# Decaying keys and queries in place in the recurrence levels, and attention maxima in one pass

## The chip, the cores and the metric

The kernel runs on one core of a Trainium2 chip. The metric is the device time of one execution in microseconds. Three runs of the kernel before gave 2209.01, 2213.13 and 2214.48 us; the median is 2213.13.

## The reference

Two layers over 512 latent and 256 context tokens (768 columns in all), width 1024, all in float32. Each layer has three token mixers in parallel (pooling windows, attention with 8 query and 2 key heads, and a gated recurrence in both directions), a gated merge, an output projection and a feed-forward part. The change touches the recurrence and the maxima of the attention.

```python
def hgrn_scan(q, k, v, log_f, s0):
    # S_t = diag(f_t) S_{t-1} + k_t v_t^T,  o_t = S_t^T q_t,  k_t = 1 - f_t
    ...
    diff = G[:, :, :, None] - G[:, :, None, :]
    decay = jnp.exp(jnp.where(mask, diff, -jnp.inf))
    A = jnp.einsum('bnthk,bnshk,bntshk->bnhts', q, k, decay)
    o_intra = jnp.einsum('bnhts,bnshv->bnthv', A, v)
    ...

def _attend(q, k, v):
    s = jnp.einsum('bqhgd,bshd->bhgqs', q, k).astype(jnp.float32) * (HEAD_DIM ** -0.5)
    p = jax.nn.softmax(s, axis=-1).astype(v.dtype)
    return jnp.einsum('bhgqs,bshd->bqhgd', p, v)
```

Softmax does not change when the same number is taken from all scores of a row, so the maximum that is subtracted need not be exact.

## The kernel before, in words

Features lie on the 128 partitions and tokens along the columns, so a tile of one feature block is 128x768 (layer 0, all tokens) or 128x512 (layer 1, which needs outputs for latent tokens only). Large products are done in three matmuls, since each operand is split into a high and a low half (`load_w`, L243 for the low half of a weight; `gemm_h`, L261).

**The recurrence** (`hgrn`, L390 on) runs twice per layer, once for each pair of heads. It builds the decayed product of queries and keys inside chunks of 128 tokens level by level: `LEVELS` are the half-block lengths h = 1, 2, 4, ..., 64. At a level, the tokens of the two halves of each block of 2h see each other through the decay between them. Four state tiles, `Pf`, `Sf`, `Pb` and `Sb`, hold prefix and suffix products of the gates f in both directions. Per level:

- GpSimd forms the decayed keys `K` from the two directions (L436, L437), VectorE the decayed queries `Q` (L439, L440);
- TensorE (PE below) multiplies them per chunk and head (`scores`, L421) into PSUM tiles of the pool `pa`, tag `att`, of which there are four;
- VectorE copies the result under a mask into `AT` (L442);
- the states are extended to the next block length in place (L448), `Sf` and `Pb` on GpSimd, `Pf` and `Sb` on VectorE.

After the last level keys and queries are multiplied with the finished states, transposed, and summed into the chunk states `st`.

**The order.** PE's order is the order in which the program is written. Between two levels the program calls `fill(F)`: it takes work from a queue of generators (projections, pooling windows' products, gates and branch products of the merge, and in layer 0 the conditioning product `ada_group`, L173) until a credit of F microseconds is used. `PACE['hg']` holds F for both layers: 1.8 and 2.2. After each head pair `finish` empties what the next one needs, or all. The order of VectorE, ScalarE and GpSimd comes from a scheduler. Each call of `fill` also lets one step of the pooling windows onto VectorE (`windows`, L531 to L552).

**Attention** (`attn_max`, L599 on, and `attn_pv`). Row maxima come from an extra pass of scores per head: for each block of 128 queries a matmul with the high half `khh` of the keys and one with the low half `kll` (L618 for context keys, 256 columns; L626 for latent keys, 512 columns), and a reduction on VectorE (L619, L627). The pass of a head is spread over the value loop of the head before it; the first head of each of the two key heads has its pass ahead of that loop.

Of the kernel before, what the change touches and what calls it, by code (L numbers as in the profile page):

```python
# [39 lines left out]
PACE = {'hn': 3.5, 'gap': (6.4, 10.2), 'hg': (1.8, 2.2), 'att': (0.7, 0.24), 'head': (2.0, 0.6), 'mid': (1.0, 0.88), 'last': (1.0, 0.7), 'tail': (7.0, 5.0)}  # L40


class Trunk:
# [330 lines left out]
    def hgrn_proj(self, l, ws, full, hp, out):  # L374

        nc = self.nc
        c0 = 0 if full else LC
        for dirn in range(2):
            ps = yield from self.gemm_h(self.load_w(ws[dirn], [P, KD, P]), self.segs(True))
            k = self.t(hp, [P, T], F32, f"k{dirn}", bufs=2)  # L380
            for s0, s1, a in ps:
# [4 lines left out]
        for s0, s1, a in ps:
            nc.scalar.copy(q[:, s0:s1], a)
        out.append(q)

    def hgrn(self, l, p, kkq, full, hp, bo):  # L390
# [3 lines left out]
        F = PACE['hg'][l]  # L394

        kf, kb, q = kkq
        P_, S_ = {}, {}
        for dirn, k in ((0, kf), (1, kb)):
            f = self.t(hp, [P, T], F32, f"f{dirn}")
            e = self.t(hp, [P, T], F32, f"e{dirn}")  # L400
            if l > 0:
                col = dirn * 2 + p
                nc.vector.tensor_scalar(out=f, in0=k, scalar1=self.olb[:, 1, col:col + 1], scalar2=1.0, op0=ALU.mult, op1=ALU.add)
                nc.vector.tensor_scalar(out=k, in0=k, scalar1=self.olb[:, 0, col:col + 1], scalar2=0.0, op0=ALU.mult, op1=ALU.add)
            else:
                nc.vector.tensor_scalar(out=f, in0=k, scalar1=-1.0, scalar2=1.0, op0=ALU.mult, op1=ALU.add)
            nc.gpsimd.memset(e, 1.0)
            P_[dirn], S_[dirn] = (f if dirn == 0 else e), (e if dirn == 0 else f)
        Pf, Sf, Pb, Sb = P_[0], S_[0], P_[1], S_[1]

        AT = self.t(hp, [P, 2, NCH, P], F32, "AT")

        def scores(K, Q, evac):
            for g0 in range(ch0, NCH, 4):
                n = min(4, NCH - g0)
                pt = [self.t(self.pa, [P, 4, P], F32, "att") for _ in range(2)]
                for i in range(n):
                    sl = slice((g0 + i) * P, (g0 + i + 1) * P)
                    for hd in range(2):
                        ph = slice(64 * hd, 64 * hd + 64)  # L420
                        nc.tensor.matmul(pt[hd][:, i, :], K[ph, sl], Q[ph, sl], start=True, stop=True)  # L421
                for hd in range(2):
                    evac(AT[:, hd, g0:g0 + n], pt[hd][:, :n], n)


        K = self.t(hp, [P, T], F32, "K")
        nc.vector.tensor_add(K[:, c0:], kf[:, c0:], kb[:, c0:])
        self.fill(F + (PACE['gap'][l] if p else 0.0))
        scores(K, q, lambda o, i, n: nc.scalar.copy(o, i))
        self.fill(F)  # L430

        for li, h in enumerate(LEVELS):
            def half(X, e, s0=0):
                return X[:, s0:].rearrange("p (n e h) -> p n e h", e=2, h=h)[:, :, e, :]
# [28 lines left out]
        kts = [self.t(hp, [P, NCH, P], F32, "Q") for _ in range(2)]  # L463
# [3 lines left out]
        for dirn, src in ((0, Sf), (1, Pb)):  # L467
            for g in ((0, 4), (4, 5)) if dirn == 0 else ((3, 6), (0, 2)):
                pt = self.t(self.pa, [P, 4, P], F32, "att")
                n = g[1] - g[0]  # L470
                for i in range(n):
                    nc.tensor.transpose(pt[:, i, :], src[:, (g[0] + i) * P:(g[0] + i + 1) * P], self.ident)
                nc.scalar.copy(kts[dirn][:, g[0]:g[1], :], pt[:, :n, :])
            self.fill(1.2)
        for g in ((0, 2), (2, 4), (4, 5)):
            for dirn in range(2):
                order = orders[dirn]
                pt = self.t(self.pa, [P, 2, P], F32, "att")
                for i in range(*g):
                    nc.tensor.matmul(pt[:, i - g[0], :], kts[dirn][:, order[i], :], self.Vt[:, order[i], p * P:(p + 1) * P], start=True, stop=True)  # L480
# [24 lines left out]
        self.headnorm(on, o, c0, self.hnw[l], hp, "e0", "e1")  # L505
# [93 lines left out]
    def attn_max(self, hl, q, full, ap):  # L599
# [13 lines left out]
        for qi in range(c0 // P, NCH, 2):  # L613
            pc = self.t(self.pa, [P, 2, LC], F32, "att")
            for j in range(2):
                ql = s[:, (qi + j) * P:(qi + j + 1) * P]
                for i, kk in enumerate((khh, kll)):
                    nc.tensor.matmul(pc[:, j, :], ql, kk[:, 0:LC], start=(i == 0), stop=(i == 1))  # L618
            nc.vector.reduce_max(mx[:, 0, qi:qi + 2], pc, axis=AX.X)  # L619
            yield  # L620
            if qi >= 2:
                for j in range(2):
                    ql = s[:, (qi + j) * P:(qi + j + 1) * P]
                    pb = self.t(self.pa, [P, LX], F32, "att")
                    for i, kk in enumerate((khh, kll)):
                        nc.tensor.matmul(pb, ql, kk[:, LC:T], start=(i == 0), stop=(i == 1))  # L626
# [662 lines left out]
```

## Time and profile before

| | before |
|---|---|
| median of three runs | 2213.13 us |
| the profiled execution: time, span | 2214.6 us, 2212.7 us |
| mean granted TensorE clock | 0.986 |
| busy: PE, weight loads | 95%, 80% |
| busy: VectorE, ScalarE, GpSimd | 52%, 33%, 19% |
| chain that ended last, by engine | PE 58%, VectorE 5%, ScalarE 2%, issue 2%, GpSimd 1% |

How to read it: an engine's busy share is over the whole span, and stages differ. The recurrence takes about 115 to 265 us of the span in layer 0 and 1380 to 1515 in layer 1. [...] In the rows PE is the matmul engine, DVE is VectorE, ACT is ScalarE, POOL is GpSimd.

### The profile page before, as it was taken

The numbers are of one execution on the slowest core, as the hardware profiler recorded it, in microseconds if no ns is written. First come the engines' busy times: TensorE is split into PE (matmuls) and PEld (weight loads), VectorE is DVE, ScalarE is ACT, GpSimd is POOL, SyncE is SP. The second block draws the span as 40 slices with busy tenths as digits, with TensorE's granted clock in tenths as the row PEclk, the third lists the DMA queues.
The fourth block names the chain that finished last, engine by engine and source line by source line (L and its number), as shares of the span: only waits on it lengthen the run. The fifth ranks groups of instructions, "written<-read, shape, count | busy, mean of one in ns | idle before, by whom it ended". The sixth has DMA issues, their size and how long they took to land.

```text
span 2212.7 us, 29478 instructions
## 1 busy us (share of the span) xinstructions
PE 2105.9 (95%) x12044; PEld 1777.2 (80%) x12044; DVE 1156.4 (52%) x1645; ACT 728.2 (33%) x1032; POOL 424.5 (19%) x383
## 2 busy tenths in 40 slices
PE   5988889999999999999999999889999899999999
PEld 4877678778888888888888889768776689888887
DVE  5377624656644557434424354985757556333333
ACT  5313123355543332112112234123555435222221
POOL 1164201342432100000000001660343421000000
PEclk9999999999999999999999999999999999999999
DMA  7202363212126135325422222113312162322322
GB/s 281 80 20 91 112 217 103 68 64 82 59 98 210 57 126 168 126 72 162 150 74 96 91 81 79 47 58 110 115 48 86 66 196 78 102 97 93 98 94 97
DMA packets 75175, 229.69 MB, mean 104 GB/s; under 512 B 8400, under 2 KB 8544, under 8 KB 74912
## 3 DMA queue, kind: packets, MB, share of 16 engines
q1 hardware_dynamic: 74592, 226.26, 30.9%
q8 instruction: 95, 1.56, 0.3%
q0 software_dynamic: 448, 1.54, 0.2%
q14 instruction: 40, 0.33, 0.0%
HBM read 208.50 MB, written 19.27 MB: 103 GB/s over the span
## 4 chain that ended last, share of the span: by engine, by line
PE 58%; DVE 5%; issue 2%; ACT 2%; POOL 1%; POOLq 0%; DVEq 0%; ACTq 0%
PE g L261 45%; PE g L1064 5%; PE g L1020 2%; PE att L1064 2%; PE att L367 1%; POOL el L682 1%; DVE lo L243 1%; PE att L700 1%; PE att L1020 1%; DVE AT L442 1%; PE att L626 1%; DVE f L448 1%; DVE nsq L318 0%; ACT hi L241 0%; PE att L672 0%
## 5 line engine op out<-in xcount | busy, mean ns | idle before, releaser
L261 PE MATMUL g<-h,hi 128*128 128x512 f32 (+1 forms) x3840 | 990.3, 359 | 10.6 <-ACT h L319 2.6
L261 PEld LDWEIGHTS g<-h,hi 128*128 128x128 f32 x3840 | 682.9, 190 | 129.5 <-issue 9.4
L261 PE MATMUL g<-h,lo 128*128 128x512 f32 (+1 forms) x1920 | 570.8, 355 | 0.0
L241 ACT CAST hi<-raw 128x1024 fp32r<-128x1024 f32 (+1 forms) x237 | 245.5, 1037 | 883.4 <-PE g L261 546.3
L243 DVE TENSOR_TENSOR lo<-raw,hi 128x1024 fp32r<-128x1024 f32 (+1 forms) x237 | 294.7, 1245 | 299.1 <-ACT hi L241 297.1
L261 PEld LDWEIGHTS g<-h,lo 128*128 128x128 f32 x1920 | 364.5, 190 | 53.0 <-issue 1.2
L324 POOL TENSOR_TENSOR h<-nsq,h 128x256 fp32r<-128x256 f32 (+1 forms) x32 | 34.3, 1075 | 732.1 <-ACT nsq L323 732.0
L682 POOL TENSOR_TENSOR el<-e,eh 128x512 fp32r<-128x512 f32 x104 | 139.6, 1346 | 149.2 <-ACT eh L679 81.0
L261 PE MATMUL g<-uh,hi 128*128 128x512 f32 (+1 forms) x416 | 129.8, 358 | 0.0
L261 PE MATMUL g<-ul,hi 128*128 128x512 f32 (+1 forms) x416 | 129.8, 358 | 0.0
L261 PE MATMUL g<-uh,lo 128*128 128x512 f32 (+1 forms) x416 | 129.8, 358 | 0.0
L1078 DVE SCALAR_TENSOR_TENSOR x<-g,mod,x 128x256 f32<-128x256 f32 (+1 forms) x64 | 42.4, 682 | 165.1 <-PE g L261 145.0
L980 DVE TENSOR_TENSOR sa<-sa,g 128x512 f32<-128x512 f32 (+1 forms) x43 | 35.1, 818 | 163.9 <-PE g L261 162.7
L214 DVE SCALAR_TENSOR_TENSOR junk<-adar,cb 128x1024 f32<-128x1024 f32 x64 | 78.2, 1222 | 37.0 <-DMA adar<-in_w_adaT_dram 36.2
L677 ACT ACTIVATE e<-att 128x512 f32<-128x512 f32 x104 | 62.0, 596 | 95.7 <-PE att L673 92.1
L261 PEld LDWEIGHTS g<-uh,hi 128*128 128x128 f32 x416 | 78.0, 188 | 12.3
L261 PEld LDWEIGHTS g<-ul,hi 128*128 128x128 f32 x416 | 78.0, 187 | 12.2
L261 PEld LDWEIGHTS g<-uh,lo 128*128 128x128 f32 x416 | 78.0, 187 | 12.2
L827 POOL TENSOR_TENSOR ybuf<-ybuf,tanh 128x768 f32<-128x768 f32 (+1 forms) x32 | 57.2, 1786 | 148.1 <-DVE tanh L825 92.4
L421 PE MATMUL att<-Q,K 64*128 64x128 f32 x560 | 47.2, 306 | 23.6 <-DVE Q L440 10.8
L421 PEld LDWEIGHTS att<-Q,K 64*128 64x128 f32 x560 | 40.4, 207 | 33.6 <-issue 8.2
L448 POOL TENSOR_TENSOR e<-e,f 128x384 f32<-128x384 f32 x56 | 65.3, 1184 | 5.5 <-DVE f L448 5.4
(340 smaller groups left out, 3123.0 us busy)
## 6 DMA issues: line engine op xcount, KB each, us to landing
raw<-in_w_fi_dram SPq DMA_DIRECT2D x88, 512.0 KB, 3.3
raw<-in_w_in_dram SPq DMA_DIRECT2D x84, 512.0 KB, 3.4
adar<-in_w_adaT_dram SPq DMA_DIRECT2D x48, 512.0 KB, 4.1
ada<-in_w_ada_dram SPq DMA_DIRECT2D x64, 256.0 KB, 4.3
raw<-in_w_fo_dram SPq DMA_DIRECT2D x34, 448.0 KB, 3.3
raw<-in_w_out_dram SPq DMA_DIRECT2D x18, 512.0 KB, 3.4
ada<-in_w_ada_dram SPq DMA_DIRECT2D x16, 512.0 KB, 10.2
raw<-in_w_fo_dram SPq DMA_DIRECT2D x16, 512.0 KB, 3.3
```

The lines of the kernel that those rows point to most:

```text
L214: i = nc.vector.scalar_tensor_tensor(out=junk, in0=raw, scalar=1.0, in1=cb[:, v, :], op0=ALU.mult, op1=ALU.mult, accum_out=rows[:, f, v:v ...
L241: nc.scalar.copy(hi, raw)
L243: nc.vector.tensor_sub(lo, raw, hi.bitcast(F32))
L261: nc.tensor.matmul(ps.part(s0, s1), w, x[:, s0:s1], start=(first and i == 0), stop=(last and i == 2))
L421: nc.tensor.matmul(pt[hd][:, i, :], K[ph, sl], Q[ph, sl], start=True, stop=True)
L448: eng.tensor_tensor(out=half(X, e), in0=half(X, e), in1=b, op=ALU.mult)
L677: nc.scalar.activation(e, pst, AF.Exp, scale=0.125)
L682: nc.gpsimd.tensor_sub(el, e, eh.bitcast(F32))
L827: nc.gpsimd.tensor_add(y[:, c0:], y[:, c0:], th[:, c0:])
L1020: nc.tensor.matmul(o, w[:, kk, :], self.h[x][kk][:, tg[0]:tg[1]], start=(kk == 0 and i == 0), stop=(kk == KD - 1 and i == 2))
L1064: self.nc.tensor.matmul(ps, w[:, i, :], xs[y][:, g0:g1], start=(i == 0 and k == 0), stop=(i == nk - 1 and k == 2))
L1078: self.nc.vector.scalar_tensor_tensor(out=x[:, s0:s1], in0=ps, scalar=g[:, d, v:v + 1], in1=x[:, s0:s1], op0=ALU.mult, op1=ALU.add)
```

## The change

The four state tiles are gone. Keys of both directions lie in one tile `k` (two halves), queries in one tile `qq`, and both are decayed in place from level to level by the totals of the neighbouring half block, which are kept in a small tile `tot` that is halved at each level. At each level:

- ScalarE copies the needed half of each direction's keys into `K` (L462);
- the scores read `qq` directly, through a pattern that takes alternate pieces of length h from its two halves (`pick`), with no query tile `Q` (L424);
- all scores of a level are issued ahead of its masked copies; after the first group's two masked copies stand the in-place products of the keys and queries (L452) and of the totals (L459), all on VectorE, then the second group's masked copies;
- GpSimd does nothing in the loop; the products after the last level are gone.

F is 2.9 and 2.6. The maxima leave out the matmul with `kll`, so each subtracted maximum is that of rounded keys.

```diff
-PACE = {..., 'hg': (1.8, 2.2), ...}
+PACE = {..., 'hg': (2.9, 2.6), ...}
...
+        def pick(X, s0, n, h, ph=slice(0, P)):
+            a = X[ph, 0, s0:s0 + n]
+            return bass.AP(a.tensor, a.offset, [a.ap[0], (2 * h, n // (2 * h)), (T + h, 2), (1, h)])
...
+        nc.vector.tensor_mul(qq[:, 1, c0:], q[:, c0:], f[:, 0, c0:])
+        nc.vector.tensor_mul(qq[:, 0, c0:], q[:, c0:], f[:, 1, c0:])
...
         for li, h in enumerate(LEVELS):
...
-            nc.gpsimd.tensor_mul(half(K, 0, c0), half(kf, 0, c0), half(Sf, 0, c0))
-            nc.gpsimd.tensor_mul(half(K, 1, c0), half(kb, 1, c0), half(Pb, 1, c0))
-            Q = self.t(hp, [P, T], F32, "Q")
-            nc.vector.tensor_mul(half(Q, 1, c0), half(q, 1, c0), half(Pf, 1, c0))
-            nc.vector.tensor_mul(half(Q, 0, c0), half(q, 0, c0), half(Sb, 0, c0))
-            scores(K, Q, lambda o, i, n: nc.vector.copy_predicated(o, mk.to_broadcast([P, n, P]), i))
-            upd(Sf, 0, Pf, 1, h - 1, nc.gpsimd)
-            upd(Pf, 1, Pf, 0, h - 1, nc.vector)
-            upd(Pb, 1, Sb, 0, 0, nc.gpsimd)
-            upd(Sb, 0, Sb, 1, 0, nc.vector)
+            def upd(X, e, s0, b):
+                x = X[:, s0:].rearrange("p (n e h) -> p n e h", e=2, h=h)[:, :, e, :]
+                n0 = s0 // (2 * h)
+                nc.vector.tensor_tensor(out=x, in0=x, in1=b[:, n0:].unsqueeze(2).to_broadcast([P, nb - n0, h]), op=ALU.mult)
+            def grow():
+                upd(k[:, 0], 0, 0, two[:, 0, :, 1])
+                upd(k[:, 1], 1, 0, two[:, 1, :, 0])
+                upd(qq[:, 1], 1, c0, two[:, 0, :, 0])
+                upd(qq[:, 0], 0, c0, two[:, 1, :, 1])
+                nc.vector.tensor_mul(nxt, two[:, :, :, 0], two[:, :, :, 1])
+            nc.scalar.copy(K[:, c0:].rearrange("p (n e h) -> p n e h", e=2, h=h), pick(k, c0, T - c0, h))
+            scores(plain(K), lambda ph, c: pick(qq, c * P, P, h, ph), grow, lambda o, i, n: nc.vector.copy_predicated(o, mk.to_broadcast([P, n, P]), i))
             self.fill(F)
...
-        nc.gpsimd.tensor_mul(Pb, Pb, kb)
-        nc.vector.tensor_mul(Sf, Sf, kf)
-        nc.vector.tensor_mul(Pf[:, c0:], Pf[:, c0:], q[:, c0:])
-        nc.vector.tensor_mul(Sb[:, c0:], Sb[:, c0:], q[:, c0:])
...
-                for i, kk in enumerate((khh, kll)):
-                    nc.tensor.matmul(pc[:, j, :], ql, kk[:, 0:LC], start=(i == 0), stop=(i == 1))
+                nc.tensor.matmul(pc[:, j, :], ql, khh[:, 0:LC], start=True, stop=True)
...
-                    for i, kk in enumerate((khh, kll)):
-                        nc.tensor.matmul(pb, ql, kk[:, LC:T], start=(i == 0), stop=(i == 1))
+                    nc.tensor.matmul(pb, ql, khh[:, LC:T], start=True, stop=True)
```

VectorE's order at a level of layer 0, first head pair, before: `att` tiles are the scores, `f` the states of the two directions.

```order
L439 TENSOR_TENSOR Q_1126<-hq_785,f_165_977 128x96x4
L440 TENSOR_TENSOR Q_1126<-hq_785,f_167_981 128x96x4
L448 TENSOR_TENSOR f_165_977<-f_165_977 128x96x4
L448 TENSOR_TENSOR f_167_981<-f_167_981 128x96x4
L442 COPY_PREDICATED AT_985<-masks_82,att_1087 128x512
L442 COPY_PREDICATED AT_985<-masks_82,att_1088 128x512
L442 COPY_PREDICATED AT_985<-masks_82,att_1099 128x256
L442 COPY_PREDICATED AT_985<-masks_82,att_1100 128x256
```

The query products and state updates of a level stood ahead of the masked copies of the level before it. The same place now (`lo` is a weight's low half, `pa` and `pb` are pooling windows):

```order
L452 TENSOR_TENSOR k_616<-k_616,tot_189_1106 128x96x4 x2
L243 TENSOR_TENSOR lo_1399<-raw_1395,hi_1397 128x1024
L538 TENSOR_TENSOR pa_1088<-pu_1087 128x799
L463 COPY_PREDICATED AT_978<-masks_82,att_1109 128x512
L463 COPY_PREDICATED AT_978<-masks_82,att_1110 128x512
L452 TENSOR_TENSOR qq_981<-qq_981,tot_176_1047 128x192x2 x2
L463 COPY_PREDICATED AT_978<-masks_82,att_1119 128x256
L463 COPY_PREDICATED AT_978<-masks_82,att_1120 128x256
L459 TENSOR_TENSOR tot_195_1154<-tot_189_1106 128x192
L541 TENSOR_TENSOR pb_1089<-pa_1088 128x798
L452 TENSOR_TENSOR k_616<-k_616,tot_195_1154 128x48x8 x2
```

The query update of a level (block pieces of 2) now stands behind the masked copies of its own level and ahead of the next scores; the key updates run a level or two ahead (pieces of 4 and 8 beside queries of 2).

ScalarE's order in the same loop, before: `AT` copies are the scores without decay, `hi` a weight's high half, `pu` the pooling input.

```order
L429 COPY AT_985<-att_1019 128x256
L429 COPY AT_985<-att_1020 128x256
L241 CAST hi_1479<-raw_1477 128x1024
L521 COPY pu_1149<-g_994 128x256
L521 COPY pu_1149<-g_994 128x512
L241 CAST hi_1598<-raw_1596 128x1024
```

And now, with the key copies of the levels among the casts:

```order
L439 COPY AT_978<-att_1020 128x256
L462 COPY K_1107<-k_616 128x768
L462 COPY K_1155<-k_616 128x768
L241 CAST hi_1397<-raw_1395 128x1024
L528 COPY pu_1087<-g_990 128x256
L528 COPY pu_1087<-g_990 128x512
L462 COPY K_1203<-k_616 128x768
L462 COPY K_1266<-k_616 128x768
L462 COPY K_1315<-k_616 128x768
L241 CAST hi_1481<-raw_1479 128x1024
```

Six key copies of the loop came into a queue that held casts and evacuations only; a cast that waits for PE to free a weight buffer now stands ahead of some of them.

## Rows read from the trace of the kernel before

**Rows 1.** Page, part 1: busy us, share of the span, instructions per engine.

```profile
PE 2105.9 (95%) x12044; PEld 1777.2 (80%) x12044; DVE 1156.4 (52%) x1645; ACT 728.2 (33%) x1032; POOL 424.5 (19%) x383
```

**Rows 2.** Level loops: length; PE, PEld, DVE, ACT, POOL busy (count); clock; DMA.

```profile
118.00:152.00 34.00, 28.06 (x214) 23.32 (x212) 30.46 (x46) 1.80 (x3) 30.82 (x32) 0.85 0.05 17
205.00:246.00 41.00, 28.15 (x297) 22.75 (x297) 36.38 (x54) 2.05 (x4) 27.77 (x25) 0.88 0.22 69
1390.00:1422.00 32.00, 26.71 (x183) 21.44 (x183) 30.88 (x40) 3.92 (x6) 26.32 (x30) 0.89 0.12 39
1466.00:1493.00 27.00, 21.35 (x148) 16.19 (x146) 26.40 (x34) 3.08 (x4) 23.26 (x23) 0.99 0.18 60
```

**Rows 3.** PE's waits, whole kernel: total us, times, longest.

```profile
PE att L421 <- DVE Q L440: 10.8, 8, 2.4
PE att L421 <- DVE AT L442: 7.8, 5, 2.4
```

**Rows 4.** VectorE's timeline, layer 0, first loop: start, duration, instruction.

```profile
124.39 1.38 DVE L439 TENSOR_TENSOR Q<-hq,f 128x384 f32<-128x384 f32 x1
...
130.61 0.54 DVE L439 TENSOR_TENSOR Q<-hq,f 128x384 f32<-128x384 f32 x1
131.08 0.54 DVE L440 TENSOR_TENSOR Q<-hq,f 128x384 f32<-128x384 f32 x1
...
132.48 1.21 DVE L243 TENSOR_TENSOR lo<-raw,hi 128x1024 fp32r<-128x1024 f32 x1
133.62 2.00 DVE L442 COPY_PREDICATED AT<-masks,att 128x512 f32<-128x512 uint8 x4
135.52 0.98 DVE L531 TENSOR_TENSOR pa<-pu 128x799 f32<-128x799 f32 x1
```

**Rows 5.** VectorE's timeline, level loop of layer 1, first pair.

```profile
1387.53 0.41 DVE L439 TENSOR_TENSOR Q<-hq,f 128x256 f32<-128x256 f32 x1
...
1425.44 1.34 DVE L442 COPY_PREDICATED AT<-masks,att 128x512 f32<-128x512 uint8 x2
```

**Rows 6.** PE's timeline, score products in the level loops of both layers.

```profile
135.48 1.61 PE L421 MATMUL att<-Q,K 64*128 64x128 f32 x24
...
139.30 1.95 PE L421 MATMUL att<-Q,K 64*128 64x128 f32 x24
...
217.33 0.71 PE L421 MATMUL att<-Q,K 64*128 64x128 f32 x6 [0.59 <-DVE AT L442]
...
1390.69 1.16 PE L421 MATMUL att<-Q,K 64*128 64x128 f32 x16
...
1394.73 1.16 PE L421 MATMUL att<-Q,K 64*128 64x128 f32 x16
```

**Rows 7.** Timeline of ScalarE, a copy of 128x768 in layer 0.

```profile
88.52 0.79 ACT L387 COPY hq<-g 128x768 f32<-128x768 f32 x1
```

**Rows 8.** Attention of both layers by stretch (columns as in rows 2).

```profile
380.00:760.00 380.00, 366.87 (x1990) 310.02 (x1990) 216.25 (x292) 168.41 (x242) 116.70 (x84) 1.00 0.28 93
1540.00:1790.00 250.00, 233.06 (x994) 182.11 (x993) 163.48 (x236) 128.50 (x189) 95.94 (x73) 0.98 0.27 89
```

**Rows 9.** Groups by line and shape, the low-half matmuls of the maxima.

```profile
L626 PE MATMUL att<-kll,qs 128*128 128x512 f32 x64 | 25.2, 393 | 0.0
...
L618 PE MATMUL att<-kll,qs 128*128 128x256 f32 x80 | 21.3, 288 | 0.0
```

**Rows 10.** PE's timeline, maxima of one head in layer 0.

```profile
454.93 0.28 PE L618 MATMUL att<-khh,qs 128*128 128x256 f32 x1
455.05 0.29 PE L618 MATMUL att<-kll,qs 128*128 128x256 f32 x1
...
456.80 0.39 PE L626 MATMUL att<-khh,qs 128*128 128x512 f32 x1
457.03 0.39 PE L626 MATMUL att<-kll,qs 128*128 128x512 f32 x1
```

**Rows 11.** Groups by line and shape, a reduction of the maxima.

```profile
L627 DVE TENSOR_REDUCE mx<-att 128x1 f32<-128x512 f32 x64 | 42.8, 680 | 13.2 <-PE att L626 13.0
```

More of the change, by code (lines that the diff above doesn't have):

```diff
@@ L38 @@
 O_LB = DEPTH * VECW
-PACE = {'hn': 3.5, 'gap': (6.4, 10.2), 'hg': (1.8, 2.2), 'att': (0.7, 0.24), 'head': (2.0, 0.6), 'mid': (1.0, 0.88), 'last': (1.0, 0.7), 'tail': (7.0, 5.0)}
+PACE = {'hn': 3.5, 'gap': (6.4, 10.2), 'hg': (2.9, 2.6), 'att': (0.7, 0.24), 'head': (2.0, 0.6), 'mid': (1.0, 0.88), 'last': (1.0, 0.7), 'tail': (7.0, 5.0)}
 class Trunk:
@@ L394, in hgrn, with plain, scores @@
         F = PACE['hg'][l]
[L396 to L401, printed above, removed]
-                col = dirn * 2 + p
[L403 to L409, printed above, removed]
-        AT = self.t(hp, [P, 2, NCH, P], F32, "AT")
-        def scores(K, Q, evac):
+        k, q = kkq
+        f = self.t(hp, [P, 2, T], F32, "f")
+        if l > 0:
+            for dirn in range(2):
+                col = dirn * 2 + p
+                nc.vector.tensor_scalar(out=f[:, dirn], in0=k[:, dirn], scalar1=self.olb[:, 1, col:col + 1], scalar2=1.0, op0=ALU.mult, op1=ALU.add)
+                nc.vector.tensor_scalar(out=k[:, dirn], in0=k[:, dirn], scalar1=self.olb[:, 0, col:col + 1], scalar2=0.0, op0=ALU.mult, op1=ALU.add)
+        else:
+            nc.vector.tensor_scalar(out=f, in0=k, scalar1=-1.0, scalar2=1.0, op0=ALU.mult, op1=ALU.add)
+        AT = self.t(hp, [P, 2, NCH, P], F32, "AT")
+        def plain(X):
+            return lambda ph, c: X[ph, c * P:(c + 1) * P]
+        def pick(X, s0, n, h, ph=slice(0, P)):
+            a = X[ph, 0, s0:s0 + n]
+            return bass.AP(a.tensor, a.offset, [a.ap[0], (2 * h, n // (2 * h)), (T + h, 2), (1, h)])
+        def scores(K, Q, between, evac):
+            parts = []
             for g0 in range(ch0, NCH, 4):
@@ L417, in scores @@
                 for i in range(n):
-                    sl = slice((g0 + i) * P, (g0 + i + 1) * P)
                     for hd in range(2):
                         ph = slice(64 * hd, 64 * hd + 64)
-                        nc.tensor.matmul(pt[hd][:, i, :], K[ph, sl], Q[ph, sl], start=True, stop=True)
+                        nc.tensor.matmul(pt[hd][:, i, :], K(ph, g0 + i), Q(ph, g0 + i), start=True, stop=True)
+                parts.append((g0, n, pt))
+            for gi, (g0, n, pt) in enumerate(parts):
@@ L462, in hgrn @@
+            mk = self.masks[:, li, :].unsqueeze(1)
+            K = self.t(hp, [P, T], F32, "K")
+            nc.scalar.copy(K[:, c0:].rearrange("p (n e h) -> p n e h", e=2, h=h), pick(k, c0, T - c0, h))
+            scores(plain(K), lambda ph, c: pick(qq, c * P, P, h, ph), grow, lambda o, i, n: nc.vector.copy_predicated(o, mk.to_broadcast([P, n, P]), i))
+            self.fill(F)
+            tot = nxt
+        dec = tot
         self.fill(F)
-        kts = [self.t(hp, [P, NCH, P], F32, "Q") for _ in range(2)]
+        kts = self.t(hp, [P, 2, NCH, P], F32, "f")
@@ L466, in hgrn @@
         orders = ((0, 1, 2, 3, 4, 5), (1, 0, 5, 4, 3, 2))
[L467 removed]
+        for dirn, src in ((0, k[:, 0]), (1, k[:, 1])):
             for g in ((0, 4), (4, 5)) if dirn == 0 else ((3, 6), (0, 2)):
@@ L479, in hgrn @@
                 for i in range(*g):
-                    nc.tensor.matmul(pt[:, i - g[0], :], kts[dirn][:, order[i], :], self.Vt[:, order[i], p * P:(p + 1) * P], start=True, stop=True)
+                    nc.tensor.matmul(pt[:, i - g[0], :], kts[:, dirn, order[i], :], self.Vt[:, order[i], p * P:(p + 1) * P], start=True, stop=True)
                 for i in range(*g):
```

39 lines of the change are left out of this document (18 added, 21 removed).

## The prediction

> **What bounds the kernel now.** I read the page first: PE (TensorE's matmul row) is busy 95% of the span, so only two things make this kernel shorter: less work on PE, or less time in which PE stands still or runs slow [rows 1]. Then the table by stretch. The four level loops, one per layer and head pair, are where PE stands still: it is busy 28.06 of 34, 28.15 of 41, 26.71 of 32 and 21.35 of 27 us, so it idles 5.9, 12.9, 5.3 and 5.7 us, 29.7 in all. Its granted clock falls to 0.85, 0.88, 0.89 and 0.99 there; the missing share times the stretch is 5.1, 4.9, 3.5 and 0.3 us, 13.8 in all. [...] **Waste of the loops: 43.5 us** [rows 2]. VectorE is busy 124 of these 134 us and GpSimd 108, ScalarE 11. The waits say the same: PE waits for the Q products and for the masked copies that free its PSUM buffers, both VectorE's [rows 3].
>
> VectorE is that full for a reason. The same 128x384 product takes 1.38 us at one place and 0.54 at another, and GpSimd is working on the same states beside it. Uncontended instructions follow each other in 0.47 us for a 384-wide product (131.08 less 130.61), 1.14 for a weight remainder, 1.90 for the four masked copies of a level in layer 0 [rows 4], 1.25 for the two of layer 1 and 0.34 for a 256-wide product (durations less the overlap of 0.07 to 0.09) [rows 5].
>
> **Part 1, the loops.** Removed: on GpSimd two key products and two state updates per level; on VectorE two query products and two state updates. Added: on VectorE four in-place products and a small product of block totals; on ScalarE one 128x768 copy. The masked copies stay. So VectorE has about the same work as before (3.8 us a level in layer 0 against 3.8) but nothing large on GpSimd beside it. Per loop I compare what VectorE needs from the scores of the first level to those of the last with what PE has to do there; the larger sets the time.
>
> PE: a level of layer 0 with 12 fill matmuls takes 139.30 - 135.48 = 3.82 us, of which the scores are 1.6, so a fill matmul costs 0.185; a level of layer 1 with 12 takes 4.04 [rows 6]. The new pace puts 18 fill matmuls into a level of layer 0, first pair.
>
> - Layer 0, first pair. VectorE: 6 x 1.90 masked copies, 12 query and 10 key products x 0.47, two remainders x 1.14, nine steps of the pooling windows (five of 0.9, four of about 0.5), totals 0.7: 31.2 us, and it starts 1.3 after the scores: 32.5. PE: 6 x (3.82 + 6 x 0.185) = 29.6. PE waits 2.9.
> - Layer 0, second pair. VectorE: 11.4 + 10.3 + 0.7 + one remainder, one merge product and small ones 2.4, and 1.3: 26.1. PE: 6 x (3.82 + about 1.0 of conditioning matmuls) = 28.9. PE sets the pace. But a conditioning tile holds one of four PSUM buffers, so the fourth score tile waits for a masked copy, as it does now: 0.59 us at one level [rows 6]. Six times 0.75: 4.5.
> - Layer 1, first pair. VectorE: 7.5 + 4.1 + 4.2 + 0.7 + 2.3 + windows 5.4, and 1.0: 25.2. PE: 6 x 4.04 = 24.2. PE waits 1.0.
> - Layer 1, second pair. VectorE: 7.5 + 4.1 + 3.8 + 0.6 + three remainders 3.4 + two merge products 1.2, and 1.0: 21.6. PE: 24.2. None.
>
> To all but the second loop I add 1 us, because a remainder stands ahead of the masked copies at one or two levels. Idle time left: 3.9 + 4.5 + 2.0 + 1.0 = 11.4. With clock loss in the ratio of before (13.8 to 29.7) 5.2 more: 16.6. **Gain 43.5 - 16.6 = 27 us**; its ends are 0 and 43.5 (a loss would take a new cost, bounded below).
>
> The longer fills cost nothing by themselves: the fill queue is emptied after each pair, so a matmul done in the loop is missing behind it. What they take away is cover behind the first pair; the 54 gate matmuls ahead of the second pair's first scores, 10 us, still stand against about 10 us on VectorE (head norm, f and key sum, an estimate from their widths by rows 4). No spare there.
>
> ScalarE's copy I price by its 0.79 us copy of the same shape [rows 7], and count at nothing: ScalarE is busy 1.8 to 3.9 us in a loop [rows 2], and the copy runs a level or more ahead of PE, since it needs the key updates only. Two key buffers allow that. Ahead of some copies in ScalarE's queue stand weight casts, which wait for PE to free a weight buffer; none that I find in the order waits for fill matmuls behind the scores that need the copy. If that cover were gone, 0.8 us times 28 levels, 22 us, would come onto the path.
>
> PE now reads the query operand through a pattern that jumps between two halves of a tile. No row has PE reading so. The lower end is no cost; the upper end is that the scores of a level double, 1.6 us in layer 0 and 1.16 in layer 1 [rows 6]. VectorE reads every second element, the smallest block, in 0.41 us for 256 elements [rows 5], in line with 0.54 for 384 [rows 4]; it is the nearest row, so I take no cost.
>
> [...]
>
> **Part 2, the maxima.** Removed: one of two matmuls of each maximum, 80 of 256 columns and 64 of 512 [rows 9]. In a stream the first follow each other in 0.12 us and the second in 0.23 [rows 10]: 48 x 0.12 + 32 x 0.23 = 13.1 us in layer 0 (eight heads, six and four query blocks), 32 x 0.12 + 32 x 0.23 = 11.2 in layer 1 (four and four), 24.4 in all. In layer 0 PE is busy 367 of 380 us [rows 8], so work taken from it shows. But for the two heads of eight whose maxima are taken ahead of the value loop, what is left is one matmul of 0.23 and a fill credit of 0.3 per reduction of 0.68 [rows 11]: VectorE sets the pace, and a quarter does not show. I take 10. In layer 1 PE already idles 17 of 250 us, at a clock of 0.98 [rows 8]: where it waits for softmax work of the other engines, less work of its own only lengthens the wait. I take half, 6. **Gain 16**; ends 4 and 24.4.
>
> **Sum.** The profiled execution took 2214.6 us, 1.5 over the median of 2213.1. 2214.6 - 27 - 16 = 2171.6; against the median **2170 us**. A measurement tells about 0.3%, 6.6 us, from no change.
>
> **Rivals** (times against the median)
> 1. The loops keep their waits: PE to VectorE to PE is now one chain (scores, masked copies, in-place queries, next scores), where before the Q product could run ahead. For it: VectorE is over 90% busy and keeps its work. Against: the contended durations go. Loops gain 6: 2191.
> 2. The maxima are hidden: reductions and exponents set attention's pace, 4 us remain: 2182.
> 3. Both, with nothing gained in the loops: 2209, no change.
> 4. The broken read costs one doubling at the smallest block only: 2 x 1.6 + 2 x 1.16 = 5.5 us: 2175.
> 5. **Slower:** the broken read slows the scores of every level. A doubling is 2 x 7 x 1.6 + 2 x 7 x 1.16 = 38.6 us; it decides from a factor of 2.1 on, where it eats the 43; at three the time is 2247. Against it: VectorE's rows.
> 6. All waste of the loops and all 24.4 us go: 2145.
>
> **Chances.** Forecast 0.36, rival one 0.17, two 0.13, three 0.07, four 0.11, five 0.05, six 0.11. The likeliest case's own range is 2160 to 2182. Reaching to rivals one and two, and part of the way to six, gives 2148 to 2200, with about 0.8 inside. Faster takes in all but three and five: 0.88; same 0.07; slower 0.05.
>
> **What would show it.** Right: in the loops the clock near 0.95 and idle time near 11 us; VectorE's 384-wide products near 0.55 us throughout; scores of 1.6 and 1.16 us; ScalarE's copies about 0.8; PE's waits in attention grown by less than 8 us. Wrong: scores of the smallest block, or of all, clearly longer (rivals four, five); PE waiting for the new query products as long as it now waits for Q (one); PE waiting for reductions, exponents or remainders 15 us more than now (two); PE waiting for ScalarE's copies, which I hold to be covered.

## The result and the profile after

Four runs of the changed kernel gave 2170.01 to 2178.84 us, median **2174.1 us**; four of the kernel before beside them 2209.01 to 2214.48, median 2213.4. The ratio is 0.9827, 95% interval 0.9803 to 0.9851: 39 us faster. The profiled execution took 2170.0 us (span 2168.2), the lowest of the four; the mean granted clock, as a share of full speed, rose from 0.986 to 0.993.

The page of the changed kernel, busy time of each engine:

```profile
PE 2069.9 (95%) x11900; PEld 1742.6 (80%) x11900; DVE 1113.8 (51%) x1659; ACT 747.5 (34%) x1058; POOL 287.9 (13%) x259
```

PE is 36 us less busy and still at 95%; GpSimd lost 137 us [rows 1]. The same four loops by stretch:

```profile
118.00:154.00 36.00, 32.89 (x284) 27.93 (x283) 33.63 (x66) 9.46 (x13) 4.68 (x16) 1.00 0.09 31
198.00:238.00 40.00, 36.50 (x452) 30.10 (x453) 29.35 (x64) 9.15 (x16) 0.00 (x0) 1.00 0.54 179
1358.00:1392.00 34.00, 30.55 (x222) 24.83 (x222) 30.50 (x58) 9.54 (x15) 4.88 (x11) 1.00 0.15 51
1436.00:1466.00 30.00, 30.00 (x202) 23.20 (x202) 26.99 (x52) 9.13 (x13) 0.00 (x0) 1.00 0.31 97
```

PE idles 3.1, 3.5, 3.4 and 0.0 us, 10.1 in all, where it idled 29.7, and its clock is 1.00 in all four, where it was 0.85 to 0.99 [rows 2]. VectorE's instructions in the loops, by form (count, sum and mean of one in ns):

```profile
L463 DVE COPY_PREDICATED AT<-masks,att 128x512 f32<-128x512 uint8 x56 | 37.8, 728 | 13.2 <-PE att L424 13.0
L452 DVE TENSOR_TENSOR k<-k,tot 128x384 f32<-128x384 f32 x48 | 24.8, 553 | 32.4 <-ACT K L462 31.6
L452 DVE TENSOR_TENSOR qq<-qq,tot 128x384 f32<-128x384 f32 x24 | 12.1, 544 | 0.0
L452 DVE TENSOR_TENSOR qq<-qq,tot 128x256 f32<-128x256 f32 x24 | 8.9, 411 | 0.0
```

Two forms of the kernel before, of the same 384 columns (a state update and a query product):

```profile
L448 DVE TENSOR_TENSOR f<-f 128x384 f32<-128x384 f32 x56 | 44.6, 829 | 40.2 <-POOL e L448 40.1
L439 DVE TENSOR_TENSOR Q<-hq,f 128x384 f32<-128x384 f32 x14 | 11.9, 849 | 0.0
```

A 384-wide product took 0.77 to 0.85 us in the mean (0.77 for the other query product, L440) and takes 0.55 now. All 112 products of the kernel before took 90.0 us; at the means of now, 0.55 and 0.41, they would take 57.7, an estimate. ScalarE's copies of the keys take 0.91 us (768 wide) and 0.67 (512), and no wait of PE names them.

The waits of PE in the whole span:

```profile
PE att L652 <- DVE m L649: 16.8, 8, 3.5
PE att L705 <- POOL el L687: 11.2, 15, 2.2
PE att L424 <- DVE qq L452: 6.6, 7, 1.7
PE att L424 <- DVE AT L463: 1.8, 3, 0.7
```

The first of them in the kernel before:

```profile
PE att L647 <- DVE m L644: 6.1, 7, 1.7
```

In the loops, 10.8 us for Q became 6.6 for `qq`, and 7.8 for `AT` became 1.8 [rows 3]. In attention PE's wait at the transpose of the maxima (for `m`, the maxima split into a high and a low part) has grown by 10.7 us, from 6.1 to 16.8.

The scores of the first two levels and one later, in layer 0's first pair and layer 1's second:

```profile
119.00 2.26 PE L424 MATMUL att<-qq,K 64*128 64x128 f32 x24
124.51 1.72 PE L424 MATMUL att<-qq,K 64*128 64x128 f32 x24
129.47 1.61 PE L424 MATMUL att<-qq,K 64*128 64x128 f32 x24
...
1437.78 1.59 PE L424 MATMUL att<-qq,K 64*128 64x128 f32 x16
1442.25 1.23 PE L424 MATMUL att<-qq,K 64*128 64x128 f32 x16
1446.40 1.16 PE L424 MATMUL att<-qq,K 64*128 64x128 f32 x16
```

Scores of h = 1 are longer than those of h = 4 by 0.65 and 0.43 us, those of h = 2 by 0.11 and 0.07; in both pairs of both layers, 2 x 0.76 + 2 x 0.50 = 2.5 us.

### The profile page after: what moved, and what is told of

Read it like the earlier page. It is cut to its first block, busy times and chain, and to the rows that moved or that the text cites. A ratio compares the mean times of both kernels' runs of the same rounds, so it can differ in the third digit from the quotient of the medians.

```text
span 2168.2 us, 29014 instructions
## 1 busy us (share of the span) xinstructions
PE 2069.9 (95%) x11900; PEld 1742.6 (80%) x11900; DVE 1113.8 (51%) x1659; ACT 747.5 (34%) x1058; POOL 287.9 (13%) x259
## 4 chain that ended last, share of the span: by engine, by line
PE 59%; DVE 4%; ACT 2%; POOL 2%; issue 1%; DMA 0%; SPq 0%; POOLq 0%; DVEq 0%; ACTq 0%
PE g L261 46%; PE g L1069 5%; PE g L1025 2%; PE att L1069 2%; PE att L367 1%; PE att L705 1%; POOL el L687 1%; POOL ybuf L832 1%; DVE lo L243 1%; PE att L1025 1%; PE att L424 1%; ACT hi L241 0%; DVE nsq L318 0%; DVE sm L773 0%; PE att L677 0%
## 5 line engine op out<-in xcount | busy, mean ns | idle before, releaser
L243 DVE TENSOR_TENSOR lo<-raw,hi 128x1024 fp32r<-128x1024 f32 (+1 forms) x237 | 290.3, 1226 | 313.4 <-ACT hi L241 306.3
L261 PEld LDWEIGHTS g<-ul,hi 128*128 128x128 f32 x416 | 78.0, 188 | 12.2
L261 PEld LDWEIGHTS g<-uh,hi 128*128 128x128 f32 x416 | 78.0, 188 | 12.2
L261 PEld LDWEIGHTS g<-uh,lo 128*128 128x128 f32 x416 | 78.0, 187 | 12.2
L463 DVE COPY_PREDICATED AT<-masks,att 128x512 f32<-128x512 uint8 (+1 forms) x84 | 48.9, 632 | 13.2 <-PE att L424 13.0
L705 PE MATMUL att<-el,vh 128*128 128x512 f32 (+1 forms) x112 | 44.2, 407 | 11.4 <-POOL el L687 11.2
L424 PE MATMUL att<-qq,K 64*128 64x128 f32 x560 | 42.8, 292 | 8.3 <-DVE qq L452 6.6
```

The lines of the kernel that those rows point to most:

```text
L243: nc.vector.tensor_sub(lo, raw, hi.bitcast(F32))
L261: nc.tensor.matmul(ps.part(s0, s1), w, x[:, s0:s1], start=(first and i == 0), stop=(last and i == 2))
L424: nc.tensor.matmul(pt[hd][:, i, :], K(ph, g0 + i), Q(ph, g0 + i), start=True, stop=True)
L463: scores(plain(K), lambda ph, c: pick(qq, c * P, P, h, ph), grow, lambda o, i, n: nc.vector.copy_predicated(o, mk.to_broadcast([P, n, P]), i))
L705: nc.tensor.matmul(pv[:, :n], v[:, sk, vsl], y[:, u * n:(u + 1) * n], start=(first and k == 0), stop=(last and k == len(todo) - 1))
```

## Experiments

My theory after this reading: the loops gave more than I forecast and the maxima less, because PE now stands at the transposes of the maxima. The rival: the forecast's own split, 27 and 16.

**One part at a time.** First the changed kernel with the maxima as before, then the kernel before with only the maxima changed:

```diff
-                nc.tensor.matmul(pc[:, j, :], ql, khh[:, 0:LC], start=True, stop=True)
+                for i, kk in enumerate((khh, kll)):
+                    nc.tensor.matmul(pc[:, j, :], ql, kk[:, 0:LC], start=(i == 0), stop=(i == 1))
...
```

> The changed kernel with the second matmul of every maximum put back (80 of 256 columns, 64 of 512), so only the loops are changed. The changed kernel took 2174.1 us in the median, the kernel before 2213.4. By the prediction the maxima gave 16 us: 2190, and the loops 27: 24 us under the kernel before. By the stretches of the two traces the loops gave more (waste 43.5 us before, 10.0 now, less about 2.5 for slower scores) and the maxima less (24.4 us of matmuls gone, some 13 us of new idle time in attention): 2185. If the maxima are hidden (rival two): 2178. If all of their 24 us show: 2198.

> The kernel before with one matmul per maximum instead of two, its loops as they were. By the prediction 16 us faster than the kernel before: 2197. By the idle time that the changed kernel's trace shows in attention, 11 us faster: 2202. Hidden (rival two): 2209. All of it: 2189. If the two parts don't touch each other, what this run and the one with the loops alone gain adds up to the gain of the whole change, 39 us; if one takes the other's cover, the two together give more than that.

Loops alone: 2177.5 us, ratio 0.9837 (0.9821 to 0.9853), 36.5 us under the 2214.0 of the kernel before. Maxima alone: 2209.2, ratio 0.9981 (0.9970 to 0.9991), 2 to 7 us. Nearly the whole gain is the loops'; the maxima are rival two's case. PE's wait for `m` is 6.1 us with the loops alone, as before, and 17.1 with the maxima alone: its growth comes from the maxima's own edit.

**The loop's fills as before.**

```diff
-PACE = {..., 'hg': (2.9, 2.6), ...}
+PACE = {..., 'hg': (1.8, 2.2), ...}
```

> The changed kernel with the loop's fills as they were before (1.8 and 2.2 us in place of 2.9 and 2.6), so 12 fill matmuls a level in place of 18 in layer 0. If VectorE sets the pace of a level, as the prediction holds for both first pairs, the loops stay as long and the fills that are missing in them come behind: 6 matmuls x 7 x 0.185 = 7.8 us in layer 0's first pair, about 4 in its second, 2 to 3 in layer 1, and the granted clock of the loops falls from 1.00 towards 0.9, 5 us more: 2185 to 2194. If PE's own work sets the pace, the fills only change their place: 2174, idle time and clock as they are.

2178.0 us, ratio 0.9838 (0.9820 to 0.9856), not told apart from the changed kernel's. Its four loops, from the start of the plain scores (without decay) to the start of those of h = 64:

```profile
113.19:143.07 29.88, 26.74 (x248) 22.53 (x247) 25.13 (x52) 8.32 (x13) 2.50 (x9) 1.00 0.06 19
197.13:231.43 34.30, 29.23 (x345) 24.04 (x344) 27.57 (x59) 10.40 (x15) 0.00 (x0) 1.00 0.38 131
1367.36:1397.00 29.64, 26.52 (x198) 21.12 (x197) 26.18 (x52) 9.05 (x15) 2.77 (x9) 1.00 0.16 54
1435.48:1462.04 26.56, 25.65 (x183) 19.66 (x182) 24.34 (x48) 8.10 (x13) 0.00 (x0) 1.00 0.28 78
```

The same of the kernel before, which has the same fills, and the changed kernel's first loop:

```profile
114.50:151.90 37.40, 31.46 (x247) 26.39 (x247) 30.36 (x46) 3.43 (x7) 32.68 (x34) 0.86 0.04 15
202.09:248.97 46.88, 32.27 (x344) 26.43 (x344) 39.00 (x58) 5.41 (x9) 28.88 (x25) 0.89 0.31 101
1387.33:1421.53 34.20, 28.92 (x197) 23.25 (x197) 33.08 (x45) 4.53 (x8) 27.19 (x31) 0.90 0.15 47
1461.64:1492.61 30.97, 25.32 (x182) 19.35 (x182) 30.37 (x39) 4.40 (x7) 26.54 (x26) 1.00 0.16 52
```

```profile
114.09:152.31 38.22, 35.11 (x296) 29.87 (x295) 32.23 (x62) 10.85 (x17) 4.66 (x15) 1.00 0.09 28
```

With the old fills the first loop is 8.3 us shorter than with the new ones, close to the 7.8 us of fill matmuls that are missing, and the clock stays at 1.00. This does not make PE the engine that sets the pace there: between its first masked copy and its last VectorE pauses only 0.5 us in all with the new fills and 0.3 with the old ones. But its load is no fixed one. It is busy 25.1 us instead of 32.2, because side works come with the fills: in the timeline of VectorE the new fills bring eight entries of the pooling windows and two weight remainders into the loop, the old ones two and one. Against the kernel before, at the same fills, the four loops are 7.5, 12.6, 4.6 and 4.4 us shorter, 29.1 in all, and VectorE's busy time in them is 29.6 us smaller (5.2, 11.4, 6.9 and 6.0): in the sum, though not loop by loop, they shrank by what VectorE lost.

**Why VectorE lost it.** Two kernels bring GpSimd back. The first gives it the two key products of each level:

```diff
-                upd(k[:, 0], 0, 0, two[:, 0, :, 1])
-                upd(k[:, 1], 1, 0, two[:, 1, :, 0])
+                upd(k[:, 0], 0, 0, two[:, 0, :, 1], nc.gpsimd)
+                upd(k[:, 1], 1, 0, two[:, 1, :, 0], nc.gpsimd)
...
```

> The changed kernel with the two in-place key products of each level on GpSimd instead of VectorE. It has GpSimd back in the loop with half of the products that it had in the kernel before. If VectorE and GpSimd slow each other whenever both work, as I read the 1.38 us against 0.54 of the same product in the kernel before, VectorE's query products go from about 0.5 to 0.8 to 1.4 us and the loops get idle time back: 2180 to 2190, though VectorE has 48 products fewer. If VectorE's own load is the bound and GpSimd is a free helper, VectorE gets 0.94 us a level less to do, the idle 10 us of the loops shrink to about 4: 2168 to 2171.

2181.2 us, ratio 0.9854 (0.9837 to 0.9871). The time lies where contention put it, but not for that reason: VectorE's 384- and 256-wide query products (without those of the first level) kept a median of 0.48 us, since GpSimd's products fell beside masked copies and pauses. What grew most is layer 0's first loop, 38.2 to 42.1 us. There some of ScalarE's copies start up to 2.4 us later in the loop, VectorE waits 3.0 us for small window works of GpSimd, PE waits 5.5 us for `qq` instead of 3.1, and the clock is 0.96; which of these costs the 3.9 us, the run does not separate. It leaves contention open. VectorE has 4 to 7 us less to do in the second pairs, and they became no faster (40.2 and 29.1 us): VectorE's load is not the bound there.

The second puts products on GpSimd that nobody waits for (in this run and the next the clearing of the state tile `st` goes from GpSimd to VectorE besides, so that it does not queue behind them):

```diff
+            if p == 1:
+                J = self.t(hp, [P, T // 2], F32, "J")
+                for _ in range(4):
+                    nc.gpsimd.tensor_mul(J, self.hg_gate[0][:, 256:640], self.hg_gate[0][:, 384:768])
...
```

> The changed kernel with four GpSimd products of 128x384 a level in both second pairs, on tiles that nothing else in the loop touches or waits for (the clearing of the state tile behind the loop goes to VectorE, so that it does not queue behind them). If VectorE and GpSimd slow each other when both multiply, as the prediction read the 1.38 us against 0.54, the query and key products of these loops take clearly longer than 0.48 to 0.55 us, and since VectorE is busy 30 of 39.6 and 25 of 29 us there the loops grow by 3 us or more each: 2180 to 2190. If GpSimd's part in the kernel before was only that others waited for it, or that it was the one slowed, VectorE's products keep their 0.48 to 0.55 us and the time stays at 2174.

It missed its place: since nothing held them back, the products ran ahead of both second pairs, which kept 39.6 and 29.0 us. The time was 2184.0 (ratio 0.9855, 0.9838 to 0.9871). But eleven of them fell on the start of layer 1's first pair, and that loop went from 32.3 to 39.0 us. VectorE and GpSimd there:

```profile
1357.78 15.47 POOL L468 TENSOR_TENSOR J<-hgate 128x384 f32<-128x384 f32 x11
...
1362.45 2.64 DVE L452 TENSOR_TENSOR k<-k,f 128x384 f32<-128x384 f32 x2
1365.01 2.03 DVE L243 TENSOR_TENSOR lo<-raw,hi 128x1024 fp32r<-128x1024 f32 x1
1366.97 1.48 DVE L436 TENSOR_TENSOR qq<-hq,f 128x512 f32<-128x512 f32 x1
```

The same instructions in the changed kernel:

```profile
1353.34 1.02 DVE L452 TENSOR_TENSOR k<-k,f 128x384 f32<-128x384 f32 x2
1354.50 1.23 DVE L243 TENSOR_TENSOR lo<-raw,hi 128x1024 fp32r<-128x1024 f32 x1
1355.64 0.68 DVE L436 TENSOR_TENSOR qq<-hq,f 128x512 f32<-128x512 f32 x1
```

Each is 0.8 us longer beside GpSimd, at all three widths (1.32 against 0.51, 2.03 against 1.23, 1.48 against 0.68), though they share no data. So I tied such products to the levels:

```diff
+            if p == 1:
+                J = self.t(hp, [P, T // 2], F32, "J")
+                nc.gpsimd.tensor_copy(J[:, 0:12], nxt[:, :, 0:6])
+                for _ in range(3):
+                    nc.gpsimd.tensor_mul(J, self.hg_gate[0][:, 256:640], self.hg_gate[0][:, 384:768])
...
```

> As the run with GpSimd products beside the loops, but each level's three products of 128x384 now follow a copy of 12 elements of that level's new totals, so that they lie beside the levels of both second pairs, where the earlier run had them all before. That run showed beside such products 1.32 us for a key product (0.51 alone), 1.48 for a 512-wide one (0.68), 2.03 for a remainder (1.23): 0.8 us more each. If this holds in the loop, the four products of a level take 3 us more where GpSimd is busy throughout, VectorE is full (30 of 39.6 and 25 of 29 us now), and each of the two loops grows by 7 to 15 us, with clock lost besides: 2190 to 2205. If the 0.8 us fell only on the few instructions seen there, the loops stay at 39.6 and 29.0 and the time at 2174 to 2177. The copy holds up nothing but GpSimd.

2184.8 us, ratio 0.9859 (0.9837 to 0.9880). The two second loops of this kernel (the profiled execution, 2189.4 us, is the longest of its four), and below them those of the changed kernel:

```profile
197.28:241.98 44.70, 38.49 (x447) 31.47 (x446) 34.92 (x63) 11.03 (x17) 24.99 (x27) 0.92 0.45 151
1442.74:1477.82 35.08, 29.27 (x197) 22.54 (x197) 31.98 (x49) 10.24 (x15) 20.29 (x20) 1.00 0.25 76
```

```profile
195.85:235.48 39.63, 35.59 (x448) 29.22 (x447) 30.02 (x63) 11.01 (x17) 0.00 (x0) 1.00 0.51 170
1433.70:1462.71 29.01, 29.01 (x197) 22.41 (x197) 25.41 (x49) 10.24 (x15) 0.00 (x0) 1.00 0.30 90
```

They grew by 5.1 and 6.1 us, the time by 11; VectorE is busier by 4.9 and 6.6 us, idle time is back and in one the clock fell to 0.92. The growth is under my 7 to 15, because only the products that meet GpSimd pay (384-wide query products up to 1.37 us, though their median in layer 0's second loop stays at 0.56), and the masked copies do not: none takes over 0.76 us, as without GpSimd. So contention cost time here without any dependence on GpSimd: it took back 5.1 of the 12.6 us by which layer 0's second loop is shorter than before at equal fills, and 6.1 in layer 1, where 4.4 had been gained. How the rest of the 12.6 divides between the denser work of GpSimd in the kernel before (28.9 us busy, 25.0 here) and waits for its results (6.7 us of VectorE there), no run shows. The traces show 0.8 us more at three widths, nothing for the masked copies, and a copy from SBUF to SBUF that paid too (L648, 1.25 us against a median of 0.17, in the rows on `m` below); by what mechanism, no run shows.

**The broken read, at every level.**

```diff
-            scores(plain(K), lambda ph, c: pick(qq, c * P, P, h, ph), grow, ...)
+            scores(plain(K), lambda ph, c: pick(qq, c * P, P, 1, ph), grow, ...)
```

From h = 2 on the scores then multiply other queries than they should; the work is the same.

> The changed kernel with every level's scores reading the queries through the pattern of block length 1 (the reads of h = 2 to 64 then take other elements of the tile, so the masked scores of those levels hold wrong products; the work is the same). In the changed kernel's trace the 24 score matmuls of h = 1 took 2.26 us against 1.61 at h = 4 and above, 16 of them 1.58 against 1.16. If the pattern is what costs this, all 28 groups of scores take 2.26 and 1.58, and PE gets 2 x (5 x 0.65 + 0.54) + 2 x (5 x 0.42 + 0.35) = 12.5 us more: 2186. If it was something else at the first level (its place behind the plain scores, the first load of K), the later levels stay at 1.6 and 1.16 and the time at 2174. Had rival five been right, the patterns of all levels would already cost, and nothing would change either.

A late level of each layer in this kernel, and its first loop:

```profile
140.59 2.26 PE L424 MATMUL att<-qq,K 64*128 64x128 f32 x24
1465.16 1.59 PE L424 MATMUL att<-qq,K 64*128 64x128 f32 x16
```

```profile
113.65:151.89 38.24, 38.14 (x295) 32.42 (x295) 32.25 (x62) 10.25 (x17) 4.65 (x15) 1.00 0.09 28
```

All scores take 2.26 and 1.59 us, where those of h = 4 and above took 1.61 and 1.16: the pattern costs it, not the place. The time was 2180.7, ratio 0.9847 (0.9833 to 0.9862), half of the 12.5 us that PE got more. Layer 0's first loop stayed at 38.2 us, because the longer scores filled PE's 3.1 us of idle time, and layer 1's at 32.3; the two second loops grew by 2.6 and 2.0 us. So PE sets the pace of the second pairs, and VectorE that of the first.

**The wait for m.** Two cures, first the later transpose (and the same in the value loop, one value block later):

```diff
...
+            rows = self.attn_rows(0, full, ap)
+            next(rows)
             self.fill(3.0)
-            s = self.attn_rows(0, full, ap)
+            next(rows, None)
             self.fill(3.0)
...
```

> The changed kernel with attn_rows cut in two: the small VectorE chain on the maxima stays where it is, and PE's transpose of its result comes one fill (3 us of other matmuls) or one value block later. If the maxima gained little because PE, with 20 us of matmuls less, now stands at these transposes (16.8 us of waits for m, 6.1 before), most of this wait goes, 12 to 15 us: 2160 to 2163. If VectorE and ScalarE set attention's pace as a whole, so that an idle time filled here opens at the value matmuls or the next reductions, the waits only move: 2172 to 2175.

then the two copies of the chain on ScalarE:

```diff
-        nc.vector.tensor_copy(mr, mx[:, 0])
-        nc.vector.tensor_copy(m2[:, 0], mr.bitcast(F32))
+        nc.scalar.copy(mr, mx[:, 0])
+        nc.scalar.copy(m2[:, 0], mr.bitcast(F32))
```

> The changed kernel with the two small copies of the maxima chain (128x6) on ScalarE instead of VectorE. In the trace these copies take 0.17 us in the median but up to 1.30 and 1.66, each time while GpSimd's subtraction for el runs beside them. If that is what makes PE wait for m, the wait falls by about 2 us at four or five heads, 6 to 9 us in all: 2165 to 2168. If the wait is set by the reductions ahead of the chain, or if ScalarE's own queue of exponents delays the copies as much, nothing: 2174, or some us slower.

2163.1 us (ratio 0.9764, 0.9748 to 0.9779) and 2164.2 (0.9768, 0.9752 to 0.9784): each some 10 us better than the changed kernel. What the second cure acts on, in the changed kernel, VectorE and GpSimd ahead of the longest wait:

```profile
1588.46 1.27 POOL L687 TENSOR_TENSOR el<-e,eh 128x512 fp32r<-128x512 f32 x1 [0.66 <-ACT eh L684]
1588.59 1.16 DVE L634 TENSOR_TENSOR mx<-mx 128x6 f32<-128x6 f32 x1
...
1590.60 0.16 DVE L647 CAST mr<-mx 128x6 fp32r<-128x6 f32 x1
1590.76 1.26 POOL L687 TENSOR_TENSOR el<-e,eh 128x512 fp32r<-128x512 f32 x1 [1.04 <-DVE mr L647]
1590.80 1.25 DVE L648 COPY m<-mr 128x6 f32<-128x6 f32 x1
1592.08 0.17 DVE L649 TENSOR_TENSOR m<-mx,m 128x6 f32<-128x6 f32 x1
...
1592.39 0.27 PE L652 MATMUL att<-cm,m 128*12 128x128 f32 x1 [3.50 <-DVE m L649]
```

Instructions on six columns take 1.16 and 1.25 us instead of 0.16 and 0.17, and each ends within 0.03 us of the subtraction for `el` that GpSimd is doing beside it. On ScalarE the copies take 0.20 us throughout. The wait for m fell only to 12.7 and 13.6 us, less than I expected of either cure; with the first cure six transposes still wait, where eight did; the second left the subtraction L649, which still takes up to 1.58 us. With the second cure PE's wait for `el` fell besides, from 11.2 to 8.0 us. The rest of the gain in the medians I did not trace.

Both cures together, and both with the second matmul of the maxima put back:

> The changed kernel with both cures for the wait for m: the two small copies on ScalarE, and the transpose one fill or one value block later. Each alone took 10 to 11 us off the changed kernel's 2174 (2163.1 with the late transposes, 2164.2 with the copies on ScalarE). If both take away the same wait, together they give little more than one: 2160 to 2164, with the wait for m near 4 us (12.7 and 13.6 alone). If they take away different waits, or if each gives back clock, they add up: 2152 to 2156.

> The same two cures with the second matmul of every maximum put back. In the changed kernel those 24 us of matmuls were worth only 3 us (2177.5 with them, 2174.1 without). If they were worth so little because their time came back as waits for m, they are worth more where that wait is gone: this run 12 to 18 us above the run with one matmul, 2173 to 2180. If attention is paced by the other engines whatever PE does, it is 3 to 5 us above it: 2163 to 2168.

2151.5 us (ratio 0.9719, 0.9702 to 0.9736), with a wait for m of 6.1 us and a clock of 0.997; and 2172.7 (0.9806, 0.9790 to 0.9821). **The first is 23 us faster than the changed kernel and 64 faster than the one before.** The medians, all with the changed loops (the kernel before had a median of 2213.4 to 2215.5 beside them):

| | chain as it was | both cures |
|---|---|---|
| two matmuls per maximum | 2177.5 | 2172.7 |
| one matmul | 2174.1 | 2151.5 |

Either alone is worth 3 to 5 us, both together 26. The attention of layer 0 and of layer 1, from the first matmul for a maximum to the last one of a value block, in these four kernels. Loops alone (two matmuls, old chain):

```profile
386.32:613.54 227.22, 218.88 (x1168) 183.11 (x1167) 137.25 (x198) 116.15 (x176) 90.91 (x71) 0.99 0.19 66
1547.01:1720.36 173.35, 156.14 (x678) 120.51 (x676) 115.41 (x175) 88.93 (x138) 78.91 (x62) 0.99 0.20 67
```

The changed kernel (one matmul, old chain):

```profile
385.72:608.42 222.70, 208.05 (x1087) 171.70 (x1086) 135.67 (x198) 116.17 (x176) 94.21 (x71) 0.98 0.20 67
1541.42:1713.17 171.75, 148.40 (x613) 111.15 (x611) 117.93 (x175) 88.93 (x138) 76.45 (x62) 0.98 0.20 67
```

Both cures, two matmuls:

```profile
386.54:610.11 223.57, 216.70 (x1167) 182.50 (x1166) 135.27 (x182) 118.29 (x192) 90.59 (x71) 1.00 0.20 67
1544.71:1716.05 171.34, 156.57 (x678) 120.73 (x676) 112.36 (x159) 90.94 (x154) 78.00 (x62) 0.99 0.20 67
```

Both cures, one matmul:

```profile
386.04:600.49 214.45, 204.49 (x1087) 170.23 (x1086) 134.58 (x182) 118.17 (x192) 90.85 (x71) 1.00 0.21 69
1531.98:1694.04 162.06, 145.73 (x614) 109.00 (x612) 111.78 (x159) 91.24 (x154) 75.71 (x62) 1.00 0.22 71
```

With the old chain, one matmul less takes 10.8 and 7.7 us off PE and puts 6.3 and 6.1 us of idle time in their place (8.3 to 14.7, 17.2 to 23.4); the clock goes from 0.99 to 0.98 besides. With the cures the same edit takes 12.2 and 10.8 us off PE, idle time grows by 3.1 and 1.6, and the stages are 9.1 and 9.3 us shorter. Neither side yields alone, because the other then ends last.

## Why the prediction was right, point by point

The time was right (2170 against 2174, inside the range), but it is the sum of two terms that were both wrong, in opposite directions: the loops gave 36.5 us, not 27, and the maxima 3 to 4, not 16. That these errors cancel is luck; the mechanism of the loops is not.

- **Idle time left in the loops: right.** 11.4 us forecast, 10.1 measured (3.9, 4.5, 2.0, 1.0 against 3.1, 3.5, 3.4, 0.0). The ground, contended products that become short, is right too: 0.55 us throughout, and 0.8 us more beside GpSimd in two experiments.
- **Clock loss left in the loops: wrong, mis-sized.** I let it fall in the ratio of the idle time, 5.2 us left (5.3 by the ratio); no run shows that it goes by this ratio. It went to nothing: 1.00 in all four loops with idle gaps of up to 1.7 us still in them. That makes 33.4 us of waste gone instead of 27; measured for the loops alone, 36.5 (ratio interval 0.9821 to 0.9853, so 33 to 40). The 3 us over, and 2.5 more that make up for the slower scores, were gained outside the four stretches, by an estimate from the page of the loops-alone run: the clock's loss over the span fell by 17.9 us (0.986 of 2212.7 to 0.994 of 2175.6), 4.1 more than the loops' 13.8, and PE's idle time by 21.0, 1.4 more than the loops' 19.6.
- **What sets a level's pace: right, VectorE in the first pairs and PE in the second**, as the run with the broken read at every level shows. By my sums, idle time included, the loops take 33.5, 33.4, 26.2 and 25.2 us from the scores of h = 1 to those of h = 64; 33.3, 33.5, 28.2 and 24.9 were measured. Wrong is that I counted the pooling windows as a fixed load of VectorE. They come with the fills: with 12 fill matmuls a level layer 0's first loop is 8.3 us shorter.
- **Longer fills cost nothing: right**, and they bring nothing that these runs can tell, as the run with the old fills shows.
- **ScalarE's copy counted at nothing: right.** 0.91 and 0.67 us, no wait of PE for it.
- **No cost for the broken read: wrong by 2.5 us**, rival four in kind, at less than half its price: not the doubling, which no row had shown, but 1.4 times at h = 1 (2.26 against 1.61 us), and 1.07 at h = 2 (1.72 against 1.61). My nearest row, VectorE's read of every second element, said nothing about PE. Rival five fell: only the pattern of block length 1 costs this much.
- **Maxima 16 us: wrong.** They gave 3 to 4, rival two's figure; alone in the kernel before, 2 to 7. The steps that failed are the 10 us of layer 0 and the 6 of layer 1. I took PE's 367 of 380 busy us [rows 8] to mean that work taken from it shows. Only 227 of these 380 us are the attention, from 413 to 640, and there PE idled 9.1 us already. Work taken from PE showed only as far as the next limit, and that one was 4.5 us away in layer 0 and 1.6 in layer 1 (227.2 to 222.7, 173.3 to 171.8 us): the chain from reductions to transposes. I had looked for it in the reductions of two heads, and not in the small VectorE instructions that stand between GpSimd's subtractions. My own sign for it, waits in attention grown by more than 8 us, came: 10.7 for m alone.
- **Rival one**, waits kept in the loops, did not come: 6.6 us for `qq` against 10.8 for Q, and 1.8 for `AT`. Of **rival six**, all 24 us of the maxima, 21 came with the cures (2172.7 to 2151.5).

## What to carry to other kernels

Before you credit a matmul that you remove, look at the idle time that the same stage already has and ask which chain ends next; here it stood 1.6 to 4.5 us away in each layer, and the matmuls were worth 3 us without a cure of that chain and 21 with it. When VectorE is the bound and GpSimd multiplies beside it, work moved from GpSimd to VectorE can be free, as here, where VectorE's busy time in the four loops fell by 29.6 us at equal fills; and a small VectorE instruction on a critical chain was better put on ScalarE than next to a long GpSimd one (the copy L648: 0.20 us there, up to 1.66 on VectorE). Judge a change of several parts by runs of its parts: this one's forecast was right in sum and wrong in both terms.

## What the runs showed of the hardware that I had not expected

- Three VectorE products compared beside GpSimd's products did not slow in proportion, they paid a nearly fixed 0.8 us (0.51 to 1.32, 0.68 to 1.48, 1.23 to 2.03). Two instructions on six columns, beside its subtraction for `el`, paid 1.0 and 1.1 (0.16 to 1.16 and 0.17 to 1.25). Masked copies, whose data come from PSUM, paid nothing: at most 0.76 us beside GpSimd's products, and 0.76 without.
- The float32 score matmuls whose moving operand jumps to the other half of a tile at every element took 1.4 times as long (2.26 against 1.61 us for 24, 1.59 against 1.16 for 16); in runs of two elements 1.07 times (1.72 and 1.23 us), and in runs of four they took the 1.61 and 1.16 us.
- The granted clock came back to 1.00 in loops with 3 us of idle time in 36, spread over gaps of 1.7 us and less; with 5.9 in 34 it was 0.85 [rows 2]. The sum of idle time did not decide it alone: with 5.7 in 27 it was 0.99 [rows 2], with 5.8 in 35 beside GpSimd's products 1.00. The scatter between the runs went with this clock: the changed kernel's four runs took 2170.0 us at 0.993, 2173.8 and 2174.4 at 0.991, 2178.8 at 0.989.
